# A block's modulation, all but its first pieces: from matrix products on TensorE to row sums on VectorE, GpSimd and ScalarE

## The chip, the cores and the metric

The kernel runs on one core of a Trainium2 chip. It is one launch; all weights lie in HBM as fp32. The metric is the device time of a launch in microseconds (us), less being better. Engines are named as in the profile: PE is TensorE, DVE VectorE, ACT ScalarE, POOL GpSimd, and SP the engine whose queue issues most loads.

## The reference

Two layers over 256 context tokens and 256 tokens of the sequence, 1024 features. Each layer is a token mixer (a recurrence, attention and a gated MLP side by side) and a mixture of 16 experts. The modulation is the part that changes. A condition vector `c` (for the sequence) and `c_ctx` (for the context) is multiplied by a 1024 x 6144 matrix, and the six parts of 1024 are the shift, scale and gate of mixer and experts:

```python
silu_c = jax.nn.silu(c)[:, None, :]
silu_cc = jax.nn.silu(c_ctx)
for l in range(DEPTH):
    last = l == DEPTH - 1
    sh1, sc1, g1, sh2, sc2, g2 = jnp.split(silu_c @ w_ada[l] + b_ada[l], 6, axis=-1)
    sh1c, sc1c, g1c, sh2c, sc2c, g2c = jnp.split(silu_cc @ w_ada[l] + b_ada[l], 6, axis=-1)
    hl = modulate(rmsnorm(xl, norm1[l]), sh1, sc1)
    hc = modulate(rmsnorm(xc, norm1[l]), sh1c, sc1c)
    yc, yl = token_mixer(hc, hl, ..., not last)
    xl = xl + g1 * yl
    ...
```

So the modulation is a product of a matrix of 2 x 25 MB with two vectors. In the last layer the context's part is needed for the first shift and scale alone.

## The kernel before, in words

Tokens are kept feature-major: `xT` has 128 partitions, 8 chunks of features, 512 tokens. The products of the mixer take their weights in runs of rows: a unit of two blocks of 128 rows by 512 columns (512 KB) is loaded by SP into `wraw` (`Pipe.load_unit`), split by ACT into `whi`, of 12 significant bits (L102), and by DVE into the remainder `wlo` (L103), and then used in three products for each block and chunk (L88 to L90). `Pipe` loads ahead as far as its slots allow (tags `w` and `wa`, two buffers each) and splits one run of rows ahead of its use. A run of rows is 24 products.

The mixer of layer 0 goes through these stages, by the time of the profiled execution: norm and modulation (to some 42 us), attention projections, attention, gates of the recurrence and convolutions (42 to 211), the recurrence (to 322), then `gate_proj`, the gMLP and three branches, each a pair of products (`branch`, to about 600), and the output product. Route and experts of layer 0 follow, then mixer 1 from about 1008 us, and its experts from about 1428.

The modulation is worked off piece by piece. The shift and scale of layer 0's mixer come first, in pieces of 256 columns, because the mixer waits for them; these stay. The others are pieces of 512 columns in a list `g.pending`: layer 0's 4 to 11 and layer 1's 0 to 7. `tick` does half a piece (L283, four blocks of 128 rows, each a product of `sc62`, the conditions' silu set among zeros, with 512 columns of weights). It is called after every run of rows from `gate_proj` on. The eight blocks of a piece add up in four row groups of one PSUM bank, `adps`, 16 rows of results for four or eight pieces. `finish` copies it out on ACT (L294), turns it feature-major by small products (L297, `adpo`) and adds the bias on DVE (L304). The weights come into slots `wa`, so `Pipe` keeps to `w` in that part (`START0`). Layer 1's pieces 8 to 11 are done in mixer 1; five half pieces are loaded and multiplied ahead of its norm (`TAIL`).

The instructions of a whole core are put in order by a scheduler ahead of the run. An engine executes its own in that order, each waiting for what it reads and for the buffer that it writes. The order of the code decides which of two is preferred, not where each ends up.

Of the kernel before, what the change touches and what calls it, by code (L numbers as in the profile page):

```python
# [23 lines left out]
KT = 8  # L24
# [21 lines left out]
LATER = 8  # L46
TAIL = 5
START1 = 8
# [10 lines left out]
START0 = 18  # L59
# [3 lines left out]
TAGS = dict(a=9, w=2, wa=2, wh=2, wl=2, h=8, t2=4, e1=2, e2=2, cz=2, b2=6)  # L63
# [36 lines left out]
def split_from(g, hi, lo, src, eng=None):  # L100
    """hi + lo == src, both of 12 significant bits."""
    g.nc.scalar.activation(hi, src, AF.Copy)  # L102
    (eng or g.nc.vector).tensor_tensor(lo, src, hi.bitcast(F32), op=ALU.subtract)  # L103


class Pipe:
    """Weights in the order in which they are used: loads run ahead as far as the slots allow, splits `look` runs of rows."""
# [108 lines left out]
def sweep(nk, n, last):  # L216
    """Order of (depth, chunk): the last run of rows finishes one chunk after the other."""
# [3 lines left out]
def fm_group(g, key, K, nch, rhs, ncols, evac):  # L221
    """Feature-major output: weights stationary, activations moving."""
# [11 lines left out]
def tm_group(g, key, K, tiles, lhs, evac):  # L234
    """Token-major output: activations stationary, weights moving."""
# [10 lines left out]
def ada_load(g, l, col, w, k0, nk, tag):  # L246
    """nk row blocks of w columns of a layer's modulation weights, from block k0 on."""
# [9 lines left out]
class Ada:  # L257
    """Pieces of w columns of the modulation of a layer, for both conditions; each piece fills its own rows of a shared bank."""
# [51 lines left out]

def tick(g, n=1):
# [13 lines left out]
def norm_sums(g, xcols, width, dve_busy=False, ss=None):  # L325
    """Partial sums of squares over partitions and chunks, four side by side."""
# [14 lines left out]
def token_rstd(g, ss, ng, nt, dim, pt):  # L341
    """1/sqrt(mean(x^2) + eps), token-major."""
# [11 lines left out]
def norm_rstd(g, xcols, width, dim, ss=None, between=None):  # L354
    """1/sqrt(mean(x^2) + eps) over partitions and chunks: [P, width], the same on every partition."""
# [12 lines left out]
def modulation(g, l, which, A):  # L368
    """Scale (times the norm's weight) and shift of every feature."""
# [9 lines left out]
def norm_mixer(g, l, between=None, then=None):  # L379
    """Feature chunks of the mixer's input, split."""  # L380
# [32 lines left out]
def rotate(g, dst, src):  # L413
    """Rotary part on partitions 64-95; src carries its halves swapped on partitions 96-127."""
# [8 lines left out]
def attention_proj(g, l):  # L423
# [45 lines left out]
    def uq(gi):  # L469
        """Two chunks of two heads each, and the rotary parts of the four; returns what completes the latter."""  # L470
# [56 lines left out]
def attention(g, l, hp, qT, kT, va, yb):  # L527
    """A pair of heads; the output comes feature-major."""
# [38 lines left out]
def mlstm_gates(g, l):  # L567
# [69 lines left out]
    # three parts of 8 bits that sum to -M, 32 rows each  # L637
# [13 lines left out]
    # -mt, m_prev - M, a - M_end, m_prev - M_end  # L651
# [10 lines left out]
def conv_half(g, l, which):  # L662
    """Depthwise convolution of the queries (0) or keys (1) of the recurrence, before its silu."""
# [127 lines left out]
def gate_proj(g, l):  # L791
    """Output gate of the recurrence and both halves of the gMLP, before their activations."""
# [16 lines left out]
def group_squares(g, ms, src, tiles, eng=None):  # L809
    """Sum of squares of each 128-wide group of token-major rows."""  # L810
# [62 lines left out]
def hi_lo(g, wd, name):  # L873
    """Both parts of four chunks; narrow ones share a slot."""
# [6 lines left out]
def branch(g, l, off, yx, y, mode, yHL=None, between=None):  # L881
    """y (+)= sigmoid(h @ w_br) * (y_x @ w_p); the last one leaves y split."""
# [57 lines left out]
def mixer(g, l):  # L940
    nc = g.nc
    seq = mixer_seq(g, l)
    if l == 0:
        g.pipe = Pipe(g, lambda i: ("w", "wa")[i % 2] if i < START0 else "w", 1, ["w"])
# [7 lines left out]
    else:  # L952
        g.pipe = Pipe(g, lambda i: "w" if i < START1 else ("w", "wa")[i % 2], 1, ["w"])
        for m in seq:
            g.pipe.add_matrix(*m)
        g.pipe.load(1)
# [5 lines left out]
        g.pipe.load(2)  # L962
# [18 lines left out]
    else:  # L981
# [3 lines left out]
        g.ticking = True  # L985
# [3 lines left out]
    if l == 0:  # L989
        g.ticking = True  # L990
# [16 lines left out]
    def between(p):  # L1007
        """After each of the four products of the first branch."""
# [6 lines left out]
    def early1(p):  # L1015
        """Weights of the experts that find room while the mixer still runs."""
# [8 lines left out]
    if l:  # L1025
        g.router = router_prep(g, l)
# [27 lines left out]
    if l == 0:  # L1054
        tick(g, sum(b.left() for b in g.pending))


def first_argmax(g, o, v, vmax, shape, tag):
    """One-hot of the first maximum over the last axis (4 wide)."""
# [11 lines left out]
def router_prep(g, l):  # L1071
    """What the router needs of weights and modulation alone."""
# [6 lines left out]
    # logits = rstd * (x @ (scale * rw)) + shift @ rw + bias  # L1079
# [14 lines left out]
    # the scale on diagonals, the shift as rows on every partition  # L1094
# [25 lines left out]
def route(g, l):  # L1120
    """norm, router, top-2 choice, and the rank of each pair within its expert."""
# [15 lines left out]
    def turned(q):  # L1137
        """Scaled rows of every tile, token-major, before they are divided by their norm."""
# [27 lines left out]
    # normalised rows, token-major  # L1166
# [20 lines left out]
    # best two of every group of experts, and the best group  # L1187
# [27 lines left out]
    # rank of the chosen pairs from 1, 0 elsewhere  # L1215
# [3 lines left out]
    def weights():  # L1219
# [6 lines left out]
        # weights of the two choices  # L1226
# [25 lines left out]
def overflow_tokens(g, r, i, x):  # L1252
    """A tile of tokens, feature-major."""
# [13 lines left out]
def overflow_expert(g, l, x, e, put):  # L1267
    """One token tile through one expert (at a run-time index)."""
# [25 lines left out]
def overflow(g, l, r, cap, put_tile):  # L1294
    """Pairs past an expert's slots: every token through every expert, weighted where the pair overflowed."""
# [22 lines left out]
def moe_rows(g, r, st, cap=P):  # L1318
    """Experts of 128 slots, rows moved by indirect DMA, weights split."""
# [9 lines left out]
    def slots(e):  # L1329
        """The token in each slot of an expert (out of range where there is none)."""  # L1330
# [25 lines left out]
    def weight_planes():  # L1356
        """Three parts of 8 bits that sum to the weights."""
# [22 lines left out]
    def turned(G):  # L1380
        """The hidden rows feature-major, split."""
# [33 lines left out]
    def add_sums(k):  # L1415
        """Chunk k of the scattered rows."""
# [5 lines left out]
    def total(k, e, ps):  # L1422
        """Chunk k of the last experts, by one-hot products."""
# [85 lines left out]
def moe_chip(g, r, st, cap=64):  # L1509
    """Two experts of 64 slots side by side; rows picked and summed by one-hot products."""  # L1510
# [27 lines left out]
    def weights(oh):  # L1538
        """Weight of each slot, and its token as one-hot rows."""
# [104 lines left out]
def paired(st, key, K):  # L1644
    """The same run of rows of two experts' matrices."""
# [28 lines left out]
def stream_pairs(g):  # L1674
    """Pairs of experts: the same rows of both, one after the other."""
# [26 lines left out]
def block_kernel(ctx, tc, x_t, c_t, vecs, w_ada, w_in, w_gk, w_uq2, a_wukv, gws, gbs, w_pa, w_pb, w_pc, w_out,  # L1702
# [4 lines left out]
    g.w_ada, g.w_in, g.w_gk, g.w_uq2, g.a_wukv = w_ada, w_in, w_gk, w_uq2, a_wukv  # L1707
# [19 lines left out]
    g.sc62 = const("sc62", [P, KT, 62])  # L1727
# [33 lines left out]
    # -1e30 where the recurrence may not look  # L1761
# [14 lines left out]
    g.ada = [const(f"ada{l}", [P, 48, 2]) for l in range(2)]  # L1776
    g.brd = [dp.tile([16, P], F32, name=f"brd{l}", tag=f"brd{l}") for l in range(2)]
# [3 lines left out]
    g.pending = [Ada(g, l, range(a, b)) for l, a, b in ((0, 4, 8), (0, 8, 12), (1, 0, 4), (1, 4, LATER))]  # L1781
# [10 lines left out]
    g.pending = [Ada(g, 1, range(LATER, 12))]  # L1792
# [23 lines left out]
def host_layout(inputs):  # L1816
# [18 lines left out]
    A['w_ada'] = f('w_ada')  # L1835
# [68 lines left out]
```

## Time and profile before

| | |
|---|---|
| median of 3 runs | 1672.93 us (1672.89 to 1675.74) |
| profiled execution, first to last instruction (span) | 1671.4 us |
| mean granted clock of TensorE | 0.978 |
| PE, DVE, ACT, POOL busy | 95%, 56%, 43%, 8% of the span |
| moved by DMA | 358.28 MB, 214 GB/s in the mean |
| modulation's products (L283) on PE, whole span | 448 records, 80.3 us |

The profiled execution's own time is its span; the runs are 1.5 us above it, for what lies before the first and behind the last instruction. A product in fp32 leaves two records in the trace. Busy time of PE is the union of its records, which overlap.

### The profile page before, as it was taken

How to read it: one execution, taken by the hardware profiler on the slowest of the kernel's cores; microseconds unless marked ns; L12 is line 12 of the kernel's file. 1: busy time of each engine (PE TensorE's matmuls, PEld its weight loads, DVE VectorE, ACT ScalarE, POOL GpSimd, SP SyncE). 2: the span in 40 equal slices, each digit the busy share in tenths (PEclk: the TensorE clock that was granted, in tenths of full speed). 3: DMA queues.
4: the chain of work that ended last, by engine and by line, in shares of the span. 5: the costliest groups of instructions: out<-in, count | busy, mean ns of one | idle time of the engine just before them, and what ended most of it. 6: DMA issues, size and time to landing. Idle time of an engine off the chain costs nothing. (4 is left out here: it accounts for less than half of the span.)

```text
span 1671.4 us, 22964 instructions
## 1 busy us (share of the span) xinstructions
PE 1582.0 (95%) x8611; PEld 1136.9 (68%) x8611; DVE 933.6 (56%) x1832; ACT 712.6 (43%) x1188; POOL 134.3 (8%) x128
## 2 busy tenths in 40 slices
PE   6999999999999999798989999999999998999998
PEld 3677767755567887577767776787689997453343
DVE  3565654723333443787877987567568666132223
ACT  2444336323232232476766786535466553110102
POOL 1000000000200011411211111010002001000000
PEclk8999999999999999799999999999999999999999
DMA  9222211476666375578998997623235776999996
GB/s 320 84 65 64 64 51 53 126 224 227 216 215 206 95 232 212 166 243 306 315 348 286 350 367 242 202 75 93 64 89 163 252 239 234 316 387 386 387 386 226
DMA packets 191210, 358.28 MB, mean 214 GB/s; under 512 B 13934, under 2 KB 30894, under 8 KB 190832
## 3 DMA queue, kind: packets, MB, share of 16 engines
q1 hardware_dynamic: 184160, 341.10, 60.4%
q0 software_dynamic: 6640, 15.53, 3.4%
q8 instruction: 70, 1.15, 0.3%
q14 instruction: 52, 0.43, 0.1%
q10 hardware_dynamic: 288, 0.07, 0.0%
HBM read 351.77 MB, written 12.60 MB: 218 GB/s over the span
## 5 line engine op out<-in xcount | busy, mean ns | idle before, releaser
L103 DVE TENSOR_TENSOR wlo<-wraw,whi 128x512 fp32r<-128x512 f32 (+4 forms) x356 | 322.2, 920 | 282.0 <-ACT whi L102 257.2
L102 ACT ACTIVATE whi<-wraw 128x512 fp32r<-128x512 f32 (+4 forms) x358 | 279.9, 802 | 356.0 <-PE mm L89 286.4
L88 PE MATMUL mm<-h,whi 128*128 128x512 f32 (+1 forms) x672 | 234.1, 354 | 4.1 <-ACT h L400 3.7
L89 PE MATMUL mm<-h,whi 128*128 128x512 f32 (+1 forms) x672 | 235.0, 353 | 0.0
L90 PE MATMUL mm<-h,wlo 128*128 128x512 f32 (+1 forms) x672 | 232.5, 351 | 1.3 <-DVE wlo L103 1.2
L88 PEld LDWEIGHTS mm<-h,whi 128*128 128x128 f32 x672 | 126.7, 190 | 35.8 <-issue 8.3
L89 PEld LDWEIGHTS mm<-h,whi 128*128 128x128 f32 x672 | 127.2, 190 | 30.9 <-issue 17.2
L90 PEld LDWEIGHTS mm<-h,wlo 128*128 128x128 f32 x672 | 126.9, 189 | 28.8 <-issue 12.1
L103 DVE TENSOR_TENSOR whl<-wraw,whl 128x1024 fp32r<-128x1024 f32 (+1 forms) x110 | 115.0, 1068 | 16.7 <-ACT whl L102 16.7
L1619 PE MATMUL mm<-wraw,x 128*64 128x512 f32 x504 | 121.2, 596 | 0.0
L102 ACT ACTIVATE whl<-wraw 128x1024 fp32r<-128x1024 f32 (+1 forms) x112 | 101.0, 931 | 19.9 <-issue 8.5
L283 PE MATMUL adps<-adw,sc 128*32 128x512 f32 (+1 forms) x448 | 80.3, 551 | 10.2 <-DMA adw<-in_w_ada 10.2
L1619 PEld LDWEIGHTS mm<-wraw,x 128*64 128x64 f32 x504 | 36.7, 137 | 67.5 <-issue 63.4
L88 PE MATMUL mm<-by,whi 128*128 128x512 f32 (+1 forms) x192 | 66.1, 344 | 0.0
L90 PE MATMUL mm<-whi,h 128*128 128x512 f32 x160 | 65.7, 413 | 0.0
L90 PE MATMUL mm<-by,wlo 128*128 128x512 f32 (+1 forms) x192 | 65.5, 341 | 0.0
L89 PE MATMUL mm<-by,whi 128*128 128x512 f32 (+1 forms) x192 | 65.2, 340 | 0.0
L88 PE MATMUL mm<-whi,h 128*128 128x512 f32 x160 | 65.0, 410 | 0.1
L89 PE MATMUL mm<-wlo,h 128*128 128x512 f32 x160 | 65.1, 407 | 0.0
L1570 PE MATMUL py<-wraw,gt 128*64 128x512 f32 x256 | 63.8, 598 | 0.7 <-ACT gt L1560 0.7
L88 PE MATMUL mm<-whi,x 128*128 128x512 f32 x128 | 53.6, 420 | 8.5 <-ACT whi L102 8.4
L546 ACT ACTIVATE pr<-sc,nm 128x512 f32<-128x512 f32 (+1 forms) x48 | 29.5, 615 | 62.6 <-DVE nm L543 59.6
(447 smaller groups left out, 2941.0 us busy)
## 6 DMA issues: line engine op xcount, KB each, us to landing
wraw<-in_e_w SPq DMA_DIRECT2D x278, 512.0 KB, 8.5
wraw<-in_w_in SPq DMA_DIRECT2D x96, 512.0 KB, 3.8
adw<-in_w_ada SPq DMA_DIRECT2D x80, 512.0 KB, 4.4
wraw<-in_e_w SPq DMA_DIRECT2D x33, 1024.0 KB, 13.4
wraw<-in_e_w SPq DMA_DIRECT2D x76, 256.0 KB, 6.1
adw<-in_w_ada SPq DMA_DIRECT2D x8, 1024.0 KB, 11.8
wraw<-in_w_out SPq DMA_DIRECT2D x16, 512.0 KB, 5.2
wraw<-in_w_pb SPq DMA_DIRECT2D x8, 512.0 KB, 4.8
```

The lines of the kernel that those rows point to most:

```text
L88: nc.tensor.matmul(ps, lh, rh, start=first, stop=False)
L89: nc.tensor.matmul(ps, lh, rl, start=False, stop=False)
L90: return nc.tensor.matmul(ps, ll, rh, start=False, stop=last)
L102: g.nc.scalar.activation(hi, src, AF.Copy)
L103: (eng or g.nc.vector).tensor_tensor(lo, src, hi.bitcast(F32), op=ALU.subtract)
L283: nc.tensor.matmul(self.ps[r:r + 32, :], g.sc62[:, k, 30 - 2 * j:62 - 2 * j], raw, start=(j == 0 and k < 4), stop=(j == n - 1 and k >= 4))
L546: last = nc.scalar.activation(pr[:, 0:w], sc[:, 0:w], AF.Exp, scale=ASC, bias=nm, accum_out=rs)
L1570: nc.tensor.matmul(py[hs, :], gt[:, k, hs], raws[s][:, kk, :], start=(k == 0), stop=(k == 3))
L1619: nc.tensor.matmul(ph[w][hs, :], x[:, k, hs], raws[s][:, kk, :], start=(k == 0), stop=(k == KT - 1))
```

## The change

All of `w_ada` but the first 2048 columns of layer 0 is handed to the kernel transposed (`w_adt`: a row is one of the features that are computed, with its 1024 weights). So 128 features by 1024 weights, 512 KB, are a chunk, loaded whole into one of two buffers `ad`. `cbc` holds the two conditions, each broadcast to all partitions; 16 products and four copies make it at the start. A feature is then the sum of its row times `cbc`. `Rows.step` does a chunk: with two conditions, the first is one multiply-and-sum on DVE, the second a multiply in place on POOL, a copy with a sum on ACT, and the bias on POOL. Chunks for one condition go to DVE and to POOL and ACT in turn. There are 48 chunks for two conditions (32 of layer 0 and 16 of layer 1) and 32 for one, so 64 row sums on each way. `tick` does a chunk after each run of rows, now from the attention's projections on. The first four pairs of pieces of 256 columns stay on PE. `Pipe` uses `w` and `wa` in turn throughout; `TAIL` is gone. Comments and doc strings are taken out, so line numbers differ. The scratch space for POOL's own DMAs is set to 2048.

```diff
-LATER = 8
-TAIL = 5
-START1 = 8
-START0 = 18
-TAGS = dict(a=9, w=2, wa=2, wh=2, wl=2, h=8, t2=4, e1=2, e2=2, cz=2, b2=6)
+TAGS = dict(ad=2, a=9, w=2, wa=2, wh=2, wl=2, h=8, t2=4, e1=2, e2=2, cz=2, b2=6)
...
+class Rows:
+    def __init__(self, g, chunks):
+        self.g, self.chunks = g, list(chunks)
+        self.raws, self.k = [], 0
...
+    def load(self, n):
+        g = self.g
+        while len(self.raws) < min(n, len(self.chunks)):
+            l, j, _ = self.chunks[len(self.raws)]
+            raw = g.t([P, D], F32, "ad", "adw")
+            r = (j - 16 if l == 0 else 32 + j) * P
+            g.nc.sync.dma_start(raw, g.w_adt[r:r + P, :])
+            self.raws.append(raw)
+    def step(self):
+        g = self.g
+        nc = g.nc
+        self.load(self.k + 2)
+        l, j, conds = self.chunks[self.k]
+        raw = self.raws[self.k]
+        n = len(conds)
+        for i, s in enumerate(conds):
+            col, bias = g.ada[l][:, j, s:s + 1], g.vec[l][:, C_BADA + j:C_BADA + j + 1]
+            if (i == 1) if n == 2 else j % 2:
+                nc.gpsimd.tensor_tensor(raw, raw, g.cbc[:, s, :], op=ALU.mult)
+                acc = g.cp.tile([P, 1], F32, name="adacc", tag="adacc", bufs=2)
+                nc.scalar.activation(raw, raw, AF.Copy, accum_out=acc)
+                nc.gpsimd.tensor_tensor(col, acc, bias, op=ALU.add)
+                continue
+            out = raw if n == 1 else g.t([P, D], BF16, "t2", "prod")
+            nc.vector.tensor_tensor_reduce(out=out, in0=raw, in1=g.cbc[:, s, :], scale=1.0, scalar=bias,
+                                           op0=ALU.mult, op1=ALU.add, accum_out=col)
...
 def tick(g, n=1):
     for _ in range(n):
-        if g.pending:
-            b = g.pending[0]
-            b.step()
-            if not b.left():
-                g.pending.pop(0)
+        if g.rows.left():
+            g.rows.step()
...
-        g.pipe = Pipe(g, lambda i: ("w", "wa")[i % 2] if i < START0 else "w", 1, ["w"])
+        g.pipe = Pipe(g, lambda i: ("w", "wa")[i % 2], 1, ["w"])
...
-        g.pipe = Pipe(g, lambda i: "w" if i < START1 else ("w", "wa")[i % 2], 1, ["w"])
+        g.pipe = Pipe(g, lambda i: ("w", "wa")[i % 2], 1, ["w"])
...
-        b = g.pending[0]
-        raws = [b.load("h", i) for i in range(TAIL)]
-        for i in range(TAIL):
-            b.step(raws[i])
...
-        g.ticking = True
+    g.ticking = True
     yb, gates, conv_q, last = attention_proj(g, l)
...
-    if l == 0:
-        g.ticking = True
     smo, gv, gu = gate_proj(g, l)
...
+    if l:
+        tick(g, g.rows.left())
...
-    g.pending = [Ada(g, l, range(a, b)) for l, a, b in ((0, 4, 8), (0, 8, 12), (1, 0, 4), (1, 4, LATER))]
+    g.cbc = const("cbc", [P, 2, D])
+    for s in range(2):
+        for q in range(2):
+            pc = g.bank([P, 512], "pcc")
+            for c in range(4):
+                nc.tensor.matmul(pc[:, c * P:(c + 1) * P], g.sc62[:, q * 4 + c, 30 + s:31 + s].to_broadcast([P, P]), g.ident, start=True, stop=True)
...
+    g.rows = Rows(g, [(0, j, (0, 1)) for j in range(16, 48)] + [(1, j, (0, 1)) for j in range(16)])
...
-    g.pending = [Ada(g, 1, range(LATER, 12))]
+    g.rows = Rows(g, [(1, j, (1,)) for j in range(16, 48)])
```

The order that the scheduler gives puts all 80 chunks, the 32 of layer 1 for one condition too, into the mixer of layer 0: 36 row sums of DVE stand in the attention part, 12 in the gates and the gMLP, and 16, with 16 multiplies of POOL beside them, in the branches. Three places show it.

The first is DVE in the attention of layer 0 before: `mx` is the maximum of a row of scores `sc`, `nm` its negative, `arc` the inverse of the sum of exponentials, `pr` the exponentials themselves, `pts` their transpose.

```order
147 L543 TENSOR_SCALAR nm<-mx 128x1
148 L512 COPY va<-mm 128x2x256
149 L548 RECIPROCAL arc<-ars 128x1
150 L549 TENSOR_SCALAR pr<-pr,arc 128x512
151 L103 TENSOR_TENSOR wlo<-wraw,whi 128x1024
152 L541 TENSOR_REDUCE mx<-sc 128x1
153 L543 TENSOR_SCALAR nm<-mx 128x1
154 L548 RECIPROCAL arc<-ars 128x1
155 L549 TENSOR_SCALAR pr<-pr,arc 128x512
156 L555 COPY pts<-pt 128x512
157 L541 TENSOR_REDUCE mx<-sc 128x1
```

And after, at the same place (the fifth to sixth maximum):

```order
186 L575 TENSOR_REDUCE mx<-sc 128x1
187 L342 ISA prod,ada_132<-adw,cbc,vec_78 128x1024
188 L342 ISA ada_132 128x1
189 L577 TENSOR_SCALAR nm<-mx 128x1
190 L99 TENSOR_TENSOR wlo<-wraw,whi 128x1024
191 L582 RECIPROCAL arc<-ars 128x1
192 L583 TENSOR_SCALAR pr<-pr,arc 128x512
193 L575 TENSOR_REDUCE mx<-sc 128x1
194 L342 ISA prod,ada_132<-adw,cbc,vec_78 128x1024
195 L342 ISA ada_132 128x1
196 L577 TENSOR_SCALAR nm<-mx 128x1
197 L582 RECIPROCAL arc<-ars 128x1
```

Each row sum is two rows, the sum and the reading of the accumulator, and one now stands behind each of these maxima, ahead of the `nm` that ACT waits for.

The second is SP in the branches, before: `adw` are the modulation's weights, and `wraw` those of `Pipe`.

```order
64 L161 DMA wraw<-in_w_pc 128x2x512
65 L252 DMA adw<-in_w_ada 128x2x512 x2
66 L161 DMA wraw<-in_w_in 128x2x512
67 L252 DMA adw<-in_w_ada 128x2x512 x2
68 L161 DMA wraw<-in_w_in 128x2x512
69 L252 DMA adw<-in_w_ada 128x2x512 x2
```

And after, in the branches for one condition each:

```order
93 L323 DMA adw<-in_w_adt 128x1024 x2
94 L157 DMA wraw<-in_w_in 128x2x512
95 L323 DMA adw<-in_w_adt 128x1024 x2
96 L157 DMA wraw<-in_w_in 128x2x512
97 L323 DMA adw<-in_w_adt 128x1024 x2
98 L157 DMA wraw<-in_w_in 128x2x512
```

There were two loads of 512 KB between two of `Pipe`, and are two now; before they went into the two buffers of the tag `wa`, and now into the two of `ad`. In the branches behind this place, the order before had no more `adw`; now it goes on ten times more (rows 93 to 111).

The third is ACT in the branches, before: `sg` is the branch's sigmoid, `ev` the modulation's copy.

```order
196 L102 ACTIVATE whi<-wraw 128x1024 x4
197 L294 ACTIVATE ev<-adps 128x512
198 L102 ACTIVATE whi<-wraw 128x1024
199 L894 ACTIVATE sg<-mm 128x512 x3
200 L102 ACTIVATE whi<-wraw 128x1024
201 L894 ACTIVATE sg<-mm 128x512
202 L102 ACTIVATE whi<-wraw 128x1024 x5
```

And after:

```order
248 L338 ACTIVATE adw,adacc<-adw 128x1024
249 L98 ACTIVATE whi<-wraw 128x1024
250 L338 ACTIVATE adw,adacc<-adw 128x1024
251 L98 ACTIVATE whi<-wraw 128x1024
252 L338 ACTIVATE adw,adacc<-adw 128x1024
253 L98 ACTIVATE whi<-wraw 128x1024
254 L338 ACTIVATE adw,adacc<-adw 128x1024
255 L98 ACTIVATE whi<-wraw 128x1024
256 L928 ACTIVATE sg<-mm 128x512 x2
```

A sum that reads what POOL multiplied now stands between each two splits `whi`.

## Rows read from the trace of the kernel before

**Rows 1.** The page: busy time of each engine, share of the span, instructions

```profile
PE 1582.0 (95%) x8611; PEld 1136.9 (68%) x8611; DVE 933.6 (56%) x1832; ACT 712.6 (43%) x1188; POOL 134.3 (8%) x128
```

**Rows 2.** Busy time by stretch: attention part, then gate part

```profile
42.00:211.00 169.00, 163.63 (x840) 120.71 (x839) 100.31 (x237) 71.60 (x138) 4.05 (x2) 0.98 0.23 68
...
322.00:522.00 200.00, 194.45 (x849) 111.06 (x848) 70.37 (x107) 53.48 (x76) 13.60 (x20) 1.00 0.69 220
```

**Rows 3.** Groups of PE, 322 to 640 us (busy, mean ns | idle before)

```profile
L283 PE MATMUL adps<-adw,sc 128*32 128x512 f32 x256 | 59.0, 605 | 5.5 <-DMA adw<-in_w_ada 5.5
...
L297 PE MATMUL adpo<-lsel,ev 128*128 128x8 f32 x32 | 3.8, 245 | 0.0
```

**Rows 4.** PE in order of time (start us, us, instruction), 386 us

```profile
386.39 0.39 PE L90 MATMUL mm<-by,wlo 128*128 128x512 f32 x1
386.62 0.40 PE L88 MATMUL mm<-by,whi 128*128 128x512 f32 x1
386.95 1.05 PE L283 MATMUL adps<-adw,sc 128*32 128x512 f32 x4
387.93 0.50 PE L89 MATMUL mm<-by,whi 128*128 128x512 f32 x1
```

**Rows 5.** PE in order of time, the norm of the second mixer

```profile
1045.53 2.96 PE L283 MATMUL adps<-adw,sc 128*32 128x512 f32 x20
1048.42 1.05 PE L347 MATMUL sst<-lsel,sp 128*128 128x1 f32 x8
...
1050.38 0.82 PE L364 MATMUL rr<-ident,nrs 128*128 128x128 f32 x5
```

**Rows 6.** Busy time by stretch, after a pause of PE

```profile
1011.50:1015.00 3.50, 3.50 (x9) 2.76 (x10) 3.50 (x5) 3.50 (x6) 0.37 (x1) 0.56 0.99 336
```

**Rows 7.** Groups by form, whole span: DVE and ACT

```profile
L103 DVE TENSOR_TENSOR wlo<-wraw,whi 128x1024 fp32r<-128x1024 f32 x150 | 182.8, 1221 | 210.5 <-ACT whi L102 187.2 <-PE mm L90 22.3 <-DMA wraw<-in_e_w 0.3
L102 ACT ACTIVATE whi<-wraw 128x1024 fp32r<-128x1024 f32 x152 | 160.0, 1057 | 231.3 <-PE mm L89 199.0 <-PE mm L90 21.2 <-PE py L90 9.6
...
L546 ACT ACTIVATION_READ_ACCUMULATOR pr<-sc,nm 128x1 f32 x48 | 9.3, 194 | 0.0
```

**Rows 8.** Groups by form, whole span: POOL

```profile
L103 POOL TENSOR_TENSOR wlo<-wraw,whi 128x1024 fp32r<-128x1024 f32 x2 | 4.7, 2364 | 0.0
```

**Rows 9.** DMA issues, 140 to 640 us (KB each, median us to landing)

```profile
adw<-in_w_ada SPq DMA_DIRECT2D x62, 512.0 KB, 4.4
wraw<-in_w_in SPq DMA_DIRECT2D x42, 512.0 KB, 3.8
```

**Rows 10.** POOL and DVE in order of time, route of layer 0

```profile
681.14 0.21 DVE L1203 TENSOR_TENSOR Ek<-o,sel 128x64 f32<-128x64 f32 x1
...
682.48 1.26 POOL L1174 TENSOR_TENSOR htok<-htok,shift 128x512 f32<-128x512 f32 x1 [1.43 <-ACT htok L1173]
682.54 1.28 DVE L1203 TENSOR_TENSOR Ek<-o,sel 128x64 f32<-128x64 f32 x1
```

**Rows 11.** Groups of DVE by form, attention part

```profile
L103 DVE TENSOR_TENSOR wlo<-wraw,whi 128x1024 fp32r<-128x1024 f32 x14 | 17.1, 1224 | 10.1 <-ACT whi L102 9.7 <-PE mm L90 0.4
...
L103 DVE TENSOR_TENSOR wlo<-wraw,whi 128x512 fp32r<-128x512 f32 x8 | 6.7, 850 | 3.5 <-ACT whi L102 3.3
...
L401 DVE SCALAR_TENSOR_TENSOR h<-u,ada,h 128x256 fp32r<-128x256 f32 x8 | 3.5, 480 | 0.1
L399 DVE SCALAR_TENSOR_TENSOR u<-xT,A,rr 128x256 f32<-128x256 f32 x8 | 3.5, 477 | 0.1
```

**Rows 12.** DVE in order of time: two maxima of the softmax

```profile
143.53 0.69 DVE L541 TENSOR_REDUCE mx<-sc 128x1 f32<-128x512 f32 x1 [0.44 <-PE sc L539]
...
161.68 0.41 DVE L541 TENSOR_REDUCE mx<-sc 128x1 f32<-128x256 f32 x1
```

**Rows 13.** ACT in order of time, branches: two successive splits

```profile
549.71 1.06 ACT L102 ACTIVATE whi<-wraw 128x1024 fp32r<-128x1024 f32 x1 [4.54 <-PE mm L89]
555.18 1.06 ACT L102 ACTIVATE whi<-wraw 128x1024 fp32r<-128x1024 f32 x1 [4.40 <-PE mm L89]
```

More of the change, by code (lines that the diff above doesn't have):

```diff
@@ L308, in finish, with left @@
             i = m + 1
+class Rows:
+    def __init__(self, g, chunks):
+        self.g, self.chunks = g, list(chunks)
+        self.raws, self.k = [], 0
+    def left(self):
+        return len(self.chunks) - self.k
+    def load(self, n):
[24 more added lines that the diff above has]
+                                           op0=ALU.mult, op1=ALU.add, accum_out=col)
+        self.raws[self.k] = None
+        self.k += 1
 def tick(g, n=1):
     for _ in range(n):
-        if g.pending:
-            b = g.pending[0]
-            b.step()
-            if not b.left():
-                g.pending.pop(0)
+        if g.rows.left():
+            g.rows.step()
 def early(g):
@@ L952, in mixer @@
     else:
-        g.pipe = Pipe(g, lambda i: "w" if i < START1 else ("w", "wa")[i % 2], 1, ["w"])
+        g.pipe = Pipe(g, lambda i: ("w", "wa")[i % 2], 1, ["w"])
         for m in seq:
             g.pipe.add_matrix(*m)
-        g.pipe.load(1)
+        g.pipe.load(2)
         g.pipe.single = True
-        b = g.pending[0]
-        raws = [b.load("h", i) for i in range(TAIL)]
-        for i in range(TAIL):
-            b.step(raws[i])
-        g.pipe.load(2)
     g.h = [g.t([P, 2, T], F32R, "h") for _ in range(KT)]
@@ L1054, in mixer @@
     if l == 0:
-        tick(g, sum(b.left() for b in g.pending))
+        tick(g, g.rows.left())
 def first_argmax(g, o, v, vmax, shape, tag):
@@ L1701, in block_kernel @@
 @with_exitstack
-def block_kernel(ctx, tc, x_t, c_t, vecs, w_ada, w_in, w_gk, w_uq2, a_wukv, gws, gbs, w_pa, w_pb, w_pc, w_out,
+def block_kernel(ctx, tc, x_t, c_t, vecs, w_ada, w_adt, w_in, w_gk, w_uq2, a_wukv, gws, gbs, w_pa, w_pb, w_pc, w_out,
                  rw, rb, e_w1, e_w3, e_w2, rope, lsel, swap, out):
@@ L1706, in block_kernel @@
     g.nc, g.tc = nc, tc
-    g.w_ada, g.w_in, g.w_gk, g.w_uq2, g.a_wukv = w_ada, w_in, w_gk, w_uq2, a_wukv
+    g.w_ada, g.w_adt, g.w_in, g.w_gk, g.w_uq2, g.a_wukv = w_ada, w_adt, w_in, w_gk, w_uq2, a_wukv
     g.x_t = x_t
@@ L1726, in block_kernel @@
     cs = const("cs", [P, KT, 2], c_t, eng=nc.sync)
-    g.sc62 = const("sc62", [P, KT, 62])
+    g.sc62 = g.t([P, KT, 62], F32, "b2", "sc62")
     nc.vector.memset(g.sc62, 0.0)
@@ L1776, in block_kernel @@
     g.ada = [const(f"ada{l}", [P, 48, 2]) for l in range(2)]
+    nc.gpsimd.memset(g.ada[1][:, 16:48, 0:1], 0.0)
     g.brd = [dp.tile([16, P], F32, name=f"brd{l}", tag=f"brd{l}") for l in range(2)]
@@ L1779, in block_kernel @@
     g.fsum = dp.tile([512, D], F32, name="fsum", tag="fsum")
-    g.pending = [Ada(g, l, range(a, b)) for l, a, b in ((0, 4, 8), (0, 8, 12), (1, 0, 4), (1, 4, LATER))]
+    g.cbc = const("cbc", [P, 2, D])
[4 more added lines that the diff above has]
+                nc.tensor.matmul(pc[:, c * P:(c + 1) * P], g.sc62[:, q * 4 + c, 30 + s:31 + s].to_broadcast([P, P]), g.ident, start=True, stop=True)
+            dst = g.cbc[:, s, q * 512:(q + 1) * 512]
+            if q:
+                nc.vector.tensor_copy(dst, pc)
+            else:
+                nc.scalar.activation(dst, pc, AF.Copy)
+    g.rows = Rows(g, [(0, j, (0, 1)) for j in range(16, 48)] + [(1, j, (0, 1)) for j in range(16)])
     with tc.tile_pool(name="mx0", bufs=1) as g.sp:
@@ L1834, in host_layout @@
     A['vecs'] = vecs.transpose(0, 2, 1)
-    A['w_ada'] = f('w_ada')
+    A['w_ada'] = f('w_ada')[0:1, :, 0:2 * D]
+    wt = f('w_ada').transpose(0, 2, 1)
+    A['w_adt'] = np.concatenate([wt[0, 2 * D:], wt[1]], axis=0)
     w_in = f('w_in')
@@ L1892 @@
     from concourse.bass_utils import run_bass_kernel_spmd as _run
-    nc = _bacc.Bacc("TRN2", target_bir_lowering=False, num_devices=1)
+    nc = _bacc.Bacc("TRN2", target_bir_lowering=False, num_devices=1, dynamic_dma_scratch_size=2048)
     arrays, args = {}, []
```

## The prediction

> **What bounds the kernel now.** I read the page's busy times first, then the same by stage, then the groups of instructions of the stage that the change empties, and then, at single places, the order in time. PE works 95% of the span [rows 1]. In the first layer's mixer it is nearly never free: 163.6 of 169 us in the attention part and 194.5 of 200 us in the gate part, while DVE has 100.3 and 70.4 us of work there [rows 2]. So in the gate part PE's own instructions are the time, and among them the modulation counts 256 records of 59.0 us with 5.5 us of waiting for its weights, and 3.8 us of the small products that turn it [rows 3]. It adds to the stream instead of lying beside it: the products of the branch start every 0.23 us (386.39, 386.62), but with one group of four records between them the next comes 1.31 us later (386.62, 387.93) [rows 4], so a group costs 1.08 us, about what it is busy. In the attention part there is no such record from 42 us on: the work moved there takes nothing away.
>
> **What it removes.** In mixer 0: 59.0 + 5.5 + 3.8 = 68.3 us of PE [rows 3], and as PE is the stage's clock, the time falls by the same. Bounds: 59 (the waits move to another load) and 70. I take −68.
>
> In mixer 1 the modulation of the last pieces goes too. At its start PE runs 20 such records for 2.96 us, and the small product `sst` of the norm stands behind them, from 1048.42; four more stand ahead of `rr` at 1050.38 [rows 5]. That is at most 2.96 + 0.9 us here, and groups further on cost 1.08 each where products stand behind them; I put the gain at −5 us. Against it: those records are the only thing PE does while the norm waits. [...] Net −3.5, bounds −7 and +2.
>
> **What it adds, by price.** A row sum on DVE reads as much as the split `wlo` of 1024 columns: 1.22 us; its second instruction reads an accumulator, nearest to ScalarE's 0.19 us row: together 1.4. The multiply on POOL is nearest to its own 128x1024 subtraction, 2.36 us. ScalarE's copy with a sum is the 1024-column activation, 1.06, plus 0.19 [rows 7, 8]. A load of 512 KB lands after 3.8 to 4.4 us [rows 9]. For 64 of each: DVE +90, ACT +80, POOL +151 us. No engine is full by that in the mean (DVE has 934 of 1671 us [rows 1]). The question is the places.
>
> *Attention part, 36 chunks.* The order of DVE sets 36 row sums into it, before, between and after a maximum and its scale of the softmax, with POOL's 36 multiplies beside them. Two limits. First, POOL and DVE do not run freely beside each other. While POOL multiplies 128x512 from 682.48 for 1.26 us, DVE's `Ek`, a product of two SBUF tiles that took 0.21 us just before, takes 1.28 [rows 10]: it ends as POOL ends. [...] Counted: POOL 36 x 2.36 = 85 us, row sums 36 x 1.4 = 50, and the largest DVE groups with two SBUF tiles, two of splits and `h` (17.1 + 6.7 + 3.5 [rows 11]), 27: 162 of 169 us. That just fits, if order were free: lower bound 0. If every DVE instruction were held up, 100.3 + 50 + 85 = 235 us, 66 more than the stage has. Second, there are two buffers, and one is free again only after load 3.8, row sum 1.4, multiply 2.36 and ACT 1.25: 8.8 us, so two buffers pass a chunk per 4.4 us, 158 of 169 us for 36. Where the order is denser it can't follow: between the maxima that begin at 143.53 and 161.68, 18.2 us [rows 12], stand seven row sums, 31 us of buffers. A late row sum stops the maxima, scales and `wlo` splits queued behind it on DVE, and PE waits for those. Nor is the SP queue free: it holds back the `wraw` loads behind an `adw` load that waits for its buffer. I take the middle of 0 and 66, since the orders are dense in some places and PE had other matmuls to do there in none I can name: **+33**.
>
> *Gate part, 12 chunks of both conditions.* One per run of rows. A run of 24 matmuls is 5.47 us (whi to whi, [rows 13]), above 4.4; and DVE had 70.4 of 200 us [rows 2]. Hidden: +1 (0 to +5).
>
> *Branches, 32 chunks of one condition.* Two per run of rows, the odd always into the same buffer. Its loop is load 3.8, multiply 2.36, ACT 1.25: 7.4 us, against 5.47 a run [rows 13]. ScalarE is the step that couples: its order sets one sum and one `whi` split alternately, so a late sum holds the split that PE needs. Sixteen pairs: 15 x (7.4 − 5.47) = 29 us; with loads of 4.4 us and 0.1 us for each of four hand-overs it is 8.4, 44 us. What covers it: PE has a run of split weights in hand, and buffers are filled before the first, 5.5 to 11 us. So +29 − 5 = **+25** (+10 to +40). The same multiplies again block `wlo`: 2.36 + 1.4 + 1.22 of 5.47 us leaves 0.5, which speaks for the upper half.
>
> *Start.* Sixteen products broadcast the condition: `rr` shows five such records at 0.82 us [rows 5], 32 records are some 5 us at the head of PE's order, where PE waited for x until 7.5 us; three row sums of 1.4 stand between the modulate steps on DVE. +4 (0 to +9).
>
> **Sum.** −68 − 3.5 + 33 + 1 + 25 + 4 = −8.5 us. The profiled span is 1671.4, the runs' median 1672.9; the 1.5 us around it stay. 1672.9 − 8.5 = **1664**.
>
> **Rivals.**
> - *All is hidden* (0.22). PE's queue runs far enough ahead and the schedule has slack for both stages: −68 − 3.5 + 0 + 0 + 10 + 4 = −57, 1615. For it: PE waited for DVE little in the attention part, and both engines are half empty. Against it: rows 10, and the odd loop of 7.4 us in 5.47.
> - *The row sums and the pool make it slower* (0.32). One mechanism: the lock and the two buffers cost what the wide count says, +55 in the attention part, and the branch loop +38: −68 − 3.5 + 55 + 1 + 38 + 4 = +26, 1699. It decides from the point where both stalls together exceed 67 us.
> - *The row sum runs at half speed* (0.08). Of DVE's instructions with a scalar and two tensors, `h` reads two SBUF tiles and takes 480 ns for 256 columns, `u` with its second tensor in PSUM 477 [rows 11], so nothing here shows such a cost. If it came, 64 x 1.2 = 77 us more of DVE, of which 36 in the attention part meet an engine already counted full: −8.5 + 43 = +35, 1708. [...]
>
> The forecast has 0.38 for stalls that eat most of the gain (1640 to 1680). A measurement of this kernel tells about 0.2%, 3.3 us, from no change. Faster: 0.22 and 0.31 of the middle; the same: 0.10, of the middle and the edge of the slow case; slower: 0.37. Range: from inside the hidden case to the slow ones, 1612 to 1702; the likeliest alone 1642 to 1684.
>
> **What would show it.** No 128x32 records after 40 us, and the gate part (322 to 522 before) some 65 us shorter: the removal. In the attention part PE idle with DVE's `wlo` and ScalarE's steps as releasers, DVE instructions of 2 to 3 us beside a POOL multiply, and a part some 30 us longer: the lock and the buffers. In the branches `whi` 7 to 8 us apart instead of 5.5, with the sum ahead of it waiting for POOL and POOL for a load: the loop. Mixer 1's norm shorter by 3 us with a lower granted clock behind it. The prediction is wrong if PE stays over 95% busy in both, which gives the first rival, or if loads of `wraw` come late in SP's queue in the gate part too, which I count as hidden.

## The result, and the profile after

The change makes the kernel slower: 1698.94 us (median of four runs, 1693.31 to 1702.49) against 1674.01, a ratio of 1.0139 with a 95% interval of 1.011 to 1.0169. The forecast of 1664 pointed the wrong way, though the time lies inside the range of 1612 to 1702; the slow rival, 1699, is what came. The profiled execution's span is 1700.8 us.

The page's first part shows PE emptier, and DVE and POOL fuller, than in [rows 1]:

```profile
PE 1543.0 (91%) x8283; PEld 1146.8 (67%) x8283; DVE 1088.0 (64%) x1957; ACT 775.5 (46%) x1312; POOL 321.8 (19%) x257
```

The busy time by stretch (length; PE, PEld, DVE, ACT, POOL busy; granted clock; DMA) shows where. The stretches are those of the kernel after: attention (two), gates and gMLP, branches.

```profile
42.00:211.00 169.00, 135.31 (x598) 98.20 (x598) 132.44 (x200) 76.56 (x142) 72.17 (x47) 0.88 0.39 125
211.00:342.00 131.00, 115.67 (x572) 80.11 (x570) 89.63 (x173) 59.52 (x119) 38.01 (x28) 1.00 0.36 114
342.00:478.00 136.00, 121.09 (x681) 99.93 (x680) 103.58 (x187) 66.98 (x117) 51.82 (x42) 0.96 0.34 107
478.00:643.00 165.00, 144.63 (x589) 113.05 (x590) 93.08 (x104) 63.35 (x106) 51.46 (x37) 0.95 0.60 203
```

In the first stretch of the attention PE did 598 records, where it had done 840 in the same 169 us [rows 2], DVE rose from 100 to 132 us, and the granted clock fell from 0.98 to 0.88.

To place the loss I compare when one and the same instruction starts in both traces. Three serve for all kernels below: the last maximum of the softmax (DVE, the end of the attention), the last write of `ym` (DVE, the end of the gates) and the last `sg` (ACT, the end of the branches). Start times in us, and the time of the kernel:

| kernel | last maximum | last `ym` | last `sg` | time |
|---|---|---|---|---|
| before | 265.1 | 444.2 | 605.5 | 1674 |
| the change | 342.4 | 479.2 | 642.9 | 1699 |
| e1, no chunks at all | 260.7 | 380.0 | 525.0 | 1580 |
| e2, memsets in place of the multiply | 289.1 | 415.1 | 555.7 | 1615 |
| e3, no multiply | 302.0 | 419.2 | 558.2 | (read no further) |
| e4, all sums on DVE | 319.6 | 442.4 | 579.5 | 1639 |
| e5, the change, ticks late | 282.8 | 419.6 | 592.0 | 1684 |
| e6, ticks late, all sums on DVE | 277.4 | 400.6 | 539.3 | 1608 |
| e7, the same, sums behind the recurrence | 258.9 | 416.9 | 556.4 | 1638 |
| e8, chunks of one condition on DVE | 338.9 | 476.0 | 620.9 | 1679 |
| e9, chunks of two conditions on DVE | 314.5 | 436.4 | 594.6 | 1656 |
| e10, e6 with idle multiplies on POOL | 294.1 | 437.7 | 624.0 | 1696 |

The attention ends 77 us later than before, the gates give back 42, and the branches, which in e1 give back 16, cost a net 2. What then follows gives back another 8 (+29 us by the first expert product of layer 1, at 1483.7 for 1454.5).

What happens in the attention is seen in the order of time (start, duration):

```profile
182.89 2.40 POOL L336 TENSOR_TENSOR adw<-adw,cbc 128x1024 f32<-128x1024 f32 x1 [3.88 <-DVE ada L342]
...
183.07 3.30 DVE L99 TENSOR_TENSOR wlo<-wraw,whi 128x1024 fp32r<-128x1024 f32 x1
...
189.91 2.41 POOL L336 TENSOR_TENSOR adw<-adw,cbc 128x1024 f32<-128x1024 f32 x1 [3.17 <-DVE ada L342]
...
190.35 3.05 DVE L342 CUSTOM_DVE_ANT_0 prod<-adw,cbc,vec 128x1024 bf16<-128x1024 f32 x1
...
193.40 1.21 DVE L99 TENSOR_TENSOR wlo<-wraw,whi 128x1024 fp32r<-128x1024 f32 x1
193.49 3.32 POOL L336 TENSOR_TENSOR adw<-adw,cbc 128x1024 f32<-128x1024 f32 x1 [1.17 <-DVE nm L577]
...
194.71 2.38 DVE L583 TENSOR_SCALAR pr<-pr,arc 128x512 f32<-128x512 f32 x1
...
197.23 0.63 PE L586 MATMUL pt<-ident,pr 128*128 128x128 f32 x4 [2.85 <-DVE pr L583]
```

Three of DVE's instructions stand beside a multiply of POOL, and each is stretched to POOL's end and then some: a split `wlo`, 3.30 us where it takes 1.22 [rows 11]; a row sum, 3.05, where it takes 1.29 in the mean in e4, with no multiply on POOL; the scale `pr`, 2.38, where it takes 0.49 (before). The multiply itself is stretched to 3.32 where a split of DVE had begun first, at 193.40. PE's transposes wait 2.85 us for the last one. Over the attention the groups of DVE (busy, mean ns) read

```profile
L342 DVE CUSTOM_DVE_ANT_0 prod<-adw,cbc,vec 128x1024 bf16<-128x1024 f32 x36 | 53.8, 1495 | 1.6 <-DMA adw<-in_w_adt 1.5
L99 DVE TENSOR_TENSOR wlo<-wraw,whi 128x1024 fp32r<-128x1024 f32 x22 | 40.3, 1833 | 15.5 <-ACT whi L98 15.5
L583 DVE TENSOR_SCALAR pr<-pr,arc 128x512 f32<-128x512 f32 x15 | 14.6, 970 | 0.5
```

against 1224 ns for the split in [rows 11]. Waits of PE there (us in total, times, longest):

```profile
PE pt L586 <- DVE pr L583: 18.8, 13, 2.9
PE mm L86 <- DVE wlo L99: 6.7, 3, 3.3
```

### The profile page after: what moved, and what is told of

The parts are those of the page before. It is cut to its first block, busy times and chain, and to the rows that moved or that the text cites. A ratio compares the mean times of both kernels' runs of the same rounds, so it can differ in the third digit from the quotient of the medians.

```text
span 1700.8 us, 22783 instructions
## 1 busy us (share of the span) xinstructions
PE 1543.0 (91%) x8283; PEld 1146.8 (67%) x8283; DVE 1088.0 (64%) x1957; ACT 775.5 (46%) x1312; POOL 321.8 (19%) x257
## 5 line engine op out<-in xcount | busy, mean ns | idle before, releaser
L99 DVE TENSOR_TENSOR wlo<-wraw,whi 128x512 fp32r<-128x512 f32 (+4 forms) x356 | 345.5, 985 | 173.2 <-ACT whi L98 162.7
L84 PE MATMUL mm<-h,whi 128*128 128x512 f32 (+1 forms) x672 | 236.2, 357 | 12.4 <-ACT h L434 4.6
L86 PE MATMUL mm<-h,wlo 128*128 128x512 f32 (+1 forms) x672 | 236.9, 358 | 10.6 <-DVE wlo L99 10.6
L85 PE MATMUL mm<-h,whi 128*128 128x512 f32 (+1 forms) x672 | 238.0, 355 | 1.7 <-DVE h L435 1.7
L336 POOL TENSOR_TENSOR adw<-adw,cbc 128x1024 f32<-128x1024 f32 x64 | 165.3, 2585 | 212.7 <-DVE ada L342 86.5
L84 PEld LDWEIGHTS mm<-h,whi 128*128 128x128 f32 x672 | 129.3, 194 | 38.2 <-ACT h L434 6.2
L85 PEld LDWEIGHTS mm<-h,whi 128*128 128x128 f32 x672 | 130.6, 194 | 19.6 <-issue 2.9
L338 ACT ACTIVATE adw<-adw 128x1024 f32<-128x1024 f32 x64 | 67.7, 1058 | 163.0 <-POOL adw L336 163.0
L84 PE MATMUL mm<-by,whi 128*128 128x512 f32 (+1 forms) x192 | 69.6, 362 | 15.7 <-ACT sg L928 15.6
L342 DVE CUSTOM_DVE_ANT_0 prod<-adw,cbc,vec 128x1024 bf16<-128x1024 f32 x48 | 76.5, 1595 | 2.4 <-DMA adw<-in_w_adt 2.4
L85 PE MATMUL mm<-by,whi 128*128 128x512 f32 (+1 forms) x192 | 67.3, 351 | 0.0
```

Of the source, the lines that this page charges most:

```text
L84: nc.tensor.matmul(ps, lh, rh, start=first, stop=False)
L85: nc.tensor.matmul(ps, lh, rl, start=False, stop=False)
L86: return nc.tensor.matmul(ps, ll, rh, start=False, stop=last)
L336: nc.gpsimd.tensor_tensor(raw, raw, g.cbc[:, s, :], op=ALU.mult)
L338: nc.scalar.activation(raw, raw, AF.Copy, accum_out=acc)
L342: nc.vector.tensor_tensor_reduce(out=out, in0=raw, in1=g.cbc[:, s, :], scale=1.0, scalar=bias, op0=ALU.mult, op1=ALU.add, accum_out=col)
```

## Experiments

**e1: no chunks.** `Rows.left` returns 0, and the modulation of the 80 chunks is zero. The chunks' loads are left out too, 316 MB being moved instead of 358, and the router works on other values.

```diff
     def left(self):
-        return len(self.chunks) - self.k
+        return 0
```

> Leaves out all 80 chunks: the modulation behind the first pieces is set to zero, so nothing is loaded, multiplied or summed for it. Every theory: this is the size of what was removed, the term of -68 in mixer 0 and -3.5 in mixer 1, so about 1602 us. If it is above 1615, the removal was worth less than I reckoned, and the loss in the attention part is to that extent no loss.

1579.73 us, 0.9426 of before (0.939 to 0.9462): leaving the work out is worth 94 us, not 71.5. From the recurrence's last `kw` to the last `sg` the two kernels run the same products but for the modulation's (1341 and 1052 records); the stretch is 299.6 us in before and 223.4 here (busy time by stretch, before, then e1):

```profile
305.90:605.50 299.60, 293.67 (x1341) 192.50 (x1340) 113.75 (x177) 86.02 (x123) 16.62 (x23) 1.00 0.62 198
```

```profile
301.60:525.00 223.40, 222.94 (x1052) 184.47 (x1052) 111.39 (x172) 82.12 (x118) 17.18 (x23) 1.00 0.39 116
```

PE's busy time falls by 70.7 us and its idle by 5.5, together 76.2, where I took 68.3. The mixer begins 4 us earlier too (by PE's 150th record, those of the modulation and of `cbc` not counted), and mixer 1, from the first `sq` of its norm on, gives about 6. Another 6 lie between the last `sg` and that `sq`, where before has no product of the modulation; where they come from is not shown.

**e2: POOL writes, and reads nothing.** Two memsets stand for the multiply.

```diff
-                nc.gpsimd.tensor_tensor(raw, raw, g.cbc[:, s, :], op=ALU.mult)
+                nc.gpsimd.memset(raw, 0.0)
+                nc.gpsimd.memset(raw, 0.0)
```

> POOL writes zeros twice over the chunk (two memsets, together about 1.9 us) in place of the multiply by the condition; so the second condition's sums are left out of the result, while POOL is busy nearly as long, the two buffers turn nearly as slowly, and ACT and POOL still hand over in the same order. Theory of the lock (POOL's reads hold up DVE): wlo back to 1.22 us and pr to 0.48 beside POOL, the last maximum of the attention at 300 us or before instead of 342, time 1650 to 1665. Theory of the two buffers and the queues: the last maximum still past 330, time 1685 to 1695.

1614.91 us, 84 less than the change and more than the lock's own forecast gave. The last maximum starts at 289.1. In the order of time POOL is busy as before, and the split beside it takes 1.21 us:

```profile
153.29 0.95 POOL L336 MEMSET adw<- 128x1024 f32 x1 [1.80 <-DVE ada L343]
...
153.75 1.21 DVE L99 TENSOR_TENSOR wlo<-wraw,whi 128x1024 fp32r<-128x1024 f32 x1
...
154.30 0.96 POOL L337 MEMSET adw<- 128x1024 f32 x1
...
156.81 0.95 POOL L336 MEMSET adw<- 128x1024 f32 x1 [1.55 <-DVE ada L343]
156.86 1.18 DVE L584 TENSOR_SCALAR pr<-pr,arc 128x512 f32<-128x512 f32 x1
...
158.02 0.95 POOL L337 MEMSET adw<- 128x1024 f32 x1
```

The scale `pr`, with one input in SBUF, is still held up (1.18 us where it takes 0.49); the split, with two, is not (1.21 us). By group, DVE over the attention:

```profile
L343 DVE CUSTOM_DVE_ANT_0 prod<-adw,cbc,vec 128x1024 bf16<-128x1024 f32 x36 | 47.6, 1323 | 7.2 <-DMA adw<-in_w_adt 7.1
L99 DVE TENSOR_TENSOR wlo<-wraw,whi 128x1024 fp32r<-128x1024 f32 x26 | 31.7, 1221 | 14.9 <-ACT whi L98 14.5 <-DMA adw<-in_w_adt 0.3
L584 DVE TENSOR_SCALAR pr<-pr,arc 128x512 f32<-128x512 f32 x16 | 11.0, 689 | 0.5
```

The split is back at its length and the row sum at 1.32 us. The hand-overs to ACT and the two buffers stayed, and so did the number of chunks in each stage (36 row sums up to the first mark of the table, 10 more to the second and 18 to the third); only the order shifted in places. By the last `sg` the kernel is 87 us ahead of the change, so nearly all of what the change loses against it stands in this mixer and goes with the reads of POOL.

**e3: no multiply at all.** The multiply's line is taken out.

> Leaves out the multiply by the condition on POOL: ACT sums the raw weights. The lock is gone and a buffer is free 2.4 us earlier. Theory of the lock: within 8 us of the kernel with memsets. Theory of the two buffers: some 35 us faster than the kernel with memsets, as the loop falls from 8.4 to 6.4 us. Theory that the row sums on DVE alone crowd the softmax: both stay above 1685.

The time says nothing: the router, fed with other sums, overfilled experts, and the path for that ran, 12,888 us (page, groups: products of line 1302, which lie in the overflow).

```profile
L1302 PE MATMUL mm<-ow,ox 128*128 128x512 f32 x3072 | 3181.4, 1139 | 4387.6 <-DMA ow<-in_e_w 4387.6
```

Its first mixer lies ahead of that and can be read: last `sg` 558.2, within 3 us of e2. In the attention its buffers, free some 2 us earlier, gave nothing (302.0 for 289.1), so there the loop of the two buffers, without the lock, is no limit. It came 13 us later with less to do, in another order, so that much can hang on the order.

**e4: all sums on DVE.**

```diff
-            if (i == 1) if n == 2 else j % 2:
+            if False:
```

> All row sums on DVE, 128 in all, nothing of it on POOL or ACT. Theory of the lock: a row sum of 1.35 us more in place of 2.4 us of POOL that hold DVE up: DVE's instructions at their normal lengths, time 1675 to 1695, not slower than the change. Theory that DVE's load decides: 64 x 1.35 = 86 us more of it, 56 of them in the attention part, time 1720 or more.

1638.84 us, 0.9778 of before (0.9735 to 0.9822), better than either theory. With twice the row sums DVE is 54.5 us late at the last maximum, less than the 77 of the change with half of them and POOL.

**e5, e6: ticks of layer 0 from gate_proj on**, with POOL (e5) and all on DVE (e6).

```diff
-    g.ticking = True
+    g.ticking = l > 0
     yb, gates, conv_q, last = attention_proj(g, l)
...
+    g.ticking = True
     smo, gv, gu = gate_proj(g, l)
```

> The change with the ticks of layer 0 begun at gate_proj, as before the change; POOL and ACT keep their half. The order then has 12 row sums and 12 multiplies ahead of the eighth maximum of the attention and none between the others, instead of 36 by the twentieth. Theory of the lock: what it costs goes with the multiplies that stand beside a busy DVE, so the last maximum is some 25 us later than before the change (12/36 of 77) instead of 77, and the gates, where DVE has room, lose little: 1645 to 1670. Theory that the loop of two buffers limits wherever the chunks are: 1690 or more.

> Ticks from gate_proj and all sums on DVE: 24 sums ahead of the eighth maximum, the other 104 behind the attention. The kernel with all sums on DVE had 72 by the end of the attention and its last maximum 54.5 us late, so here some 18 us, and 1610 to 1635 if the gates and branches hide the rest. If DVE is then the bound there (some 1.35 us x 3 in a run of rows of 5.5 us, beside a split of 1.22), the time is that of the kernel with all sums on DVE, 1639, or more.

e5: 1683.97 us, above the forecast of 1645 to 1670. The last maximum came a little better than expected (+18 us, for some 25), but between the last `ym` and the last `sg` it took 172 us, where e1 takes 145 and the change 164. Fifteen of its multiplies stand behind the last `sg`, and from there to the end it takes 1088 us, 30 more than the change: the cost moved with the multiplies. e6: 1608.31 us, 0.9611 (0.9595 to 0.9627), the fastest kernel here that computes the modulation, 65 us below before and within 29 of leaving the work out. DVE is busy 197 of 218 us in its gates and branches while PE loses 7 (busy time by stretch, as above):

```profile
42.00:211.00 169.00, 162.87 (x816) 121.06 (x812) 120.25 (x257) 70.24 (x130) 4.18 (x2) 0.97 0.38 114
...
322.00:540.00 218.00, 211.23 (x977) 172.96 (x975) 196.67 (x316) 80.27 (x117) 23.57 (x21) 0.99 0.65 205
540.00:640.00 100.00, 84.66 (x483) 64.98 (x481) 71.08 (x178) 28.13 (x38) 23.32 (x23) 0.91 0.81 276
```

**e7: no sum ahead of the recurrence's end.** As e6, with every row sum ordered on DVE behind the recurrence's last addition.

```diff
-            nc.vector.tensor_tensor_reduce(out=out, in0=raw, ...)
+            with g.tc.issue_after(g.hold.ins):
+                nc.vector.tensor_tensor_reduce(out=out, in0=raw, ...)
```

> As the one before, but every row sum is ordered on DVE behind the recurrence's last sum of both directions, so none stands in the attention. Theory that the cost is where DVE's order holds up the softmax: the last maximum at its old place, and the time 1600 to 1625, since the work left out altogether gave 1580. If instead DVE's total after the attention decides (128 x 1.35 = 173 us for some 200 that DVE has free between 322 and 640): 1630 to 1650.

1638.02 us: the attention is as short as without the work (258.9), and behind it the lead over e6 of 18 us turns into 30 us behind. That is what the second theory had: the room there is not enough for all 128, and the 24 sums that e6 leaves in the attention were the better choice.

**e8, e9: the halves apart.**

```diff
-            if (i == 1) if n == 2 else j % 2:
+            if n == 2 and i == 1:          # e8
+            if n == 1 and j % 2:           # e9
```

> The change, but the 16 chunks of one condition that go to POOL and ACT go to DVE too; the 48 of two conditions stay as they are. Theory of the loop in the branches (load, multiply, sum on ACT, then the split that PE needs: 7.3 us where a run of rows needs 5.45): splits back to some 5.5 us apart, 20 to 30 us faster than the change, so about 1675, and the last maximum of the attention still at 342. If the branches wait for the buffers alone, less than 10 us faster.

> The counterpart: both conditions of the 48 chunks on DVE, the 32 chunks of one condition as in the change. The attention is then that of the kernel with all sums on DVE (last maximum some 55 us late instead of 77) and the branches keep their 7.3 us between splits: 1660 to 1672. The gains of the two together should come to the 60 us between the change and the kernel with all sums on DVE; if they come to much less, the two stages are not independent.

1679.15 and 1656.17 us: 19.8 and 42.8 less than the change, together 62.6, against 60.1 for e4 at once. So the two stages add up. In e8 the branches take as long as in e1 (144.9 us from the last `ym` to the last `sg`, for 145.0), in the change 163.7. In the branches of the change the loop is seen whole (start, duration):

```profile
547.03 1.06 ACT L338 ACTIVATE adw<-adw 128x1024 f32<-128x1024 f32 x1 [5.36 <-POOL adw L336]
...
548.08 1.04 ACT L98 ACTIVATE whi<-wraw 128x1024 fp32r<-128x1024 f32 x1
548.20 0.81 SPq L323 DMA_DIRECT2D adw<-in_w_adt  x2
...
551.75 2.42 POOL L336 TENSOR_TENSOR adw<-adw,cbc 128x1024 f32<-128x1024 f32 x1 [3.30 <-DMA adw<-in_w_adt]
...
553.11 2.13 DVE L342 CUSTOM_DVE_ANT_0 adw<-adw,cbc,vec 128x1024 f32<-128x1024 f32 x1 [2.72 <-DMA adw<-in_w_adt]
...
554.20 1.06 ACT L338 ACTIVATE adw<-adw 128x1024 f32<-128x1024 f32 x1 [5.07 <-POOL adw L336]
...
555.25 1.04 ACT L98 ACTIVATE whi<-wraw 128x1024 fp32r<-128x1024 f32 x1
```

Loads are issued when ACT's sum ends (548.20), POOL begins 3.5 us later, takes 2.42, ACT 1.06 and the reading, and then comes the split: 548.08 to 555.25, 7.2 us. The row sum beside it takes 2.13. In e8 the splits are at their old pace of [rows 13]:

```profile
531.02 1.07 ACT L98 ACTIVATE whi<-wraw 128x1024 fp32r<-128x1024 f32 x1 [6.15 <-PE mm L85]
536.46 1.06 ACT L98 ACTIVATE whi<-wraw 128x1024 fp32r<-128x1024 f32 x1 [4.37 <-PE mm L85]
541.90 1.06 ACT L98 ACTIVATE whi<-wraw 128x1024 fp32r<-128x1024 f32 x1 [4.38 <-PE mm L85]
```

**e10: e6 with 48 multiplies on POOL that nobody reads**, each behind both sums of its chunk, without ACT. Its sums are complete.

```diff
+        if n == 2:
+            nc.gpsimd.tensor_tensor(raw, raw, g.cbc[:, 1, :], op=ALU.mult)
         self.raws[self.k] = None
```

> The fastest kernel so far (ticks from gate_proj, all sums on DVE, 1608) with 48 multiplies added on POOL whose product nobody reads: after both sums of a chunk, the buffer is multiplied in place. ACT has no part in it. Theory of the lock: POOL's reads alone hold DVE up, 48 x 2.4 = 115 us of POOL beside a DVE that is nearly full there: 30 to 70 us slower than 1608, with splits wlo of up to 3.6 us. Theory that it was the hand-over to ACT in its fixed order: within 10 us of 1608.

1696.39 us: 88 more than e6, above the 30 to 70 expected. PE's wait for `wlo`, from 40 to 640 us, is 6.5 us in e6 and 30.4 here (waits of PE, e6, then e10), and the row sums take 1.74 us in the mean for 1.29 (groups of DVE, e6, then e10):

```profile
PE mm L86 <- DVE wlo L99: 6.5, 5, 2.4
```

```profile
PE mm L86 <- DVE wlo L99: 30.4, 15, 6.5
```

```profile
L342 DVE CUSTOM_DVE_ANT_0 prod<-adw,cbc,vec 128x1024 bf16<-128x1024 f32 x96 | 120.4, 1287 | 6.5 <-DMA adw<-in_w_adt 6.4
```

```profile
L342 DVE CUSTOM_DVE_ANT_0 prod<-adw,cbc,vec 128x1024 bf16<-128x1024 f32 x96 | 164.1, 1736 | 22.4 <-DMA adw<-in_w_adt 22.1
```

The multiply also keeps its buffer longer: these row sums wait 22.1 us for their loads, 6.4 in e6. So up to some 16 of the 88 us can be the buffers. Busy, these row sums are 44 us longer.

## Why the prediction was wrong, point by point

**The removal** (−68 and −3.5) was undersized: −94 by e1, 76 of it in the stream. I took the busy time of the records, and busy time is a union. Between the other products the 55 groups of before leave gaps of 66 us, waits included, the first product behind each takes 0.1 us longer, 5.5 together, and the small products are 3.8: 75 of the 76. Of mixer 1's part the change itself shows some 4 us (+33.6 at its first `sq`, +29.2 at the experts), as forecast, and the lower clock that I expected behind the norm: 0.78 and 0.54 granted in the two stretches of 5 us from 1080 us on, 1.00 in the 10 us after them, where before has 1.00 in every 5 us from 1040 to 1065 us. The 1.5 us that the net of −3.5 sets against the gain for such a clock were an estimate, and no run shows the term: the change shows these clocks, and the 4 us for mixer 1's part as a whole.

**The attention** (+33) is the step that failed. Against e1 the change is 82 us late at the last maximum, 11 of it from the start (71.5 for 60.6 at PE's 150th record, counted as above; I had +4), so some 71 in the attention, above my upper bound of 66. I had seen the lock in [rows 10] and counted it, and then took the middle between nothing and all of it because the order is dense in some places only. No row showed that PE could cover half, and I could name no place where it had other matmuls to do. The parts, with the start: with memsets the last maximum is 28 us later than in e1, with the multiplies 82. So about 53 are POOL's reads, and 28 the row sums in DVE's order, with ACT's copies. The two buffers, my second limit, cost little: DVE's row sums wait 1.5 us in all for their loads there (the group above), and e3 gained nothing by freeing the buffers. (I also counted seven row sums between the maxima of [rows 12]; the trace has six.) Each edit gives the scheduler another order, and e3's 13 us say how much that can be, so these parts are no better than that.

Two things that the wide count left out can be seen. The lock holds both ways: DVE stretches the multiplies, to 2.58 us in the mean (165.3 us for 64) where I had 2.36. And in the first stretch, where PE was busy for 135 us of 169 instead of 164, the granted clock was lower, 0.88 for 0.98 [rows 2]; from 211 to 342 us, with PE busy for 116 of 131, it was 1.00. A lower clock was in [rows 6], and I used it for mixer 1 alone. How many of the 71 us each is was not measured apart.

**The gates** (+1) cost 17 us against e1 (99 late at the last `ym`, 82 at the last maximum). With memsets they cost 7 (e2) and with all sums on DVE under 4 (e4), so most of it goes with the multiplies. DVE has room there, but a split that is stretched holds PE all the same: PE waits 5.7 us for `wlo` from 342 to 479 us in the change, 0.5 from 260 to 380 us in e1.

**The branches** (+25) came out at 19 (118 late at the last `sg`, 99 at the last `ym`), by the loop of 7.2 us that I had put at 7.4. Here the loop and the size were right, and e8 gives the 19 back. e2, with all sixteen chunks in this stretch too, shows the loop without POOL's reads (ACT in order of time):

```profile
483.36 1.05 ACT L98 ACTIVATE whi<-wraw 128x1024 fp32r<-128x1024 f32 x1
490.35 1.04 ACT L98 ACTIVATE whi<-wraw 128x1024 fp32r<-128x1024 f32 x1
498.59 1.04 ACT L98 ACTIVATE whi<-wraw 128x1024 fp32r<-128x1024 f32 x1
503.77 1.06 ACT L98 ACTIVATE whi<-wraw 128x1024 fp32r<-128x1024 f32 x1 [4.14 <-PE mm L85]
509.21 1.06 ACT L98 ACTIVATE whi<-wraw 128x1024 fp32r<-128x1024 f32 x1 [3.34 <-PE mm L85]
```

Ahead of the second and third of these a sum waits for POOL, and they come 7.0 and 8.2 us after the split before: the loop is there without the lock. But e2's order has at most three such splits in a row, where the change has thirteen (525.21 to 614.67, 7.5 us apart in the mean), and e2's branches take 140.6 us, no longer than e1's. How much of the 19 us is the order and how much is the lock stays open.

**The rivals.** "Row sums and pool make it slower", at 0.32, was right in the lock and the loop, and not in the two buffers; the two stalls together exceeded its bound of 67 even though the removal was larger. That its 1699 is the measured time is luck: its removal was some 22 us short, its attention 16, its gates 16 and its start 7, and its branches 19 too long. The half-speed row sum did not come: it takes 1.29 and 1.28 us in the mean in e4's two groups of row sums (96 and 32), where POOL multiplies nothing, so the row with `h` in [rows 11] told it rightly. What was held up in these traces: beside a multiply of POOL the split, with two inputs in SBUF, took 3.30 us, and beside a memset 1.21 (e2); `pr`, with one input there, took 2.38 us beside a multiply and 1.18 beside a memset, for 0.49 in before.

In steps from run to run: 94 us removed with the loads (e1); 35 for 64 row sums, copies, hand-overs and the loads (e2 less e1); 84 for POOL's reads (the change less e2, its multiply being 0.5 us longer than the memsets included). That these make the measured +25 is no proof, since each step ends where the next begins.

## What to carry to other kernels

Here an idle POOL was not free where DVE lay on a path that PE waited for: a split of 1.22 us took 3.30 beside a multiply of 2.40. Price a multiply on POOL as DVE time at the same place, and look for one instance in the trace of both running side by side before halving it. Putting all 128 sums on DVE gave 1639 us where half of them on POOL gave 1699, and starting them where DVE has room gave 1608. Price work that leaves a pipelined stream by the gap that it makes in the stream, not by its busy time: here PE's stream became 76 us shorter, where busy time and waits had come to 68.

## What the runs showed of the hardware that I had not expected

POOL's multiply and DVE stretched each other: the split took 3.30 us for 1.22, and 64 multiplies took 2.58 us in the mean in the change, 48 took 2.91 in e10, where the shortest take 2.34; e10's cost the kernel 88 us, 1.8 us each, the buffers that they hold included. In e2 a memset on POOL left a two-input split alone (1.21 us), but held a one-input scale (1.18 us for 0.49). And PE was granted 0.88 over 169 us of the change's attention, where it was busy for 135 us, and 0.97 in e6, where it was busy for 163 of the same 169 us.
